# A planner takes the small loads of a recurrence as landing far later: a hybrid GDN and RWKV-7 encoder block on one core

## The chip, the core and the metric

The kernel runs on one core of a Trainium2 chip. The core has a matrix engine (PE, with its weight loads shown apart as PEld), a vector engine (DVE), a scalar engine (ACT), a general engine (POOL) and a sync engine (SP) from which most transfers are issued. Every engine works through its own list of instructions in order and waits on semaphores where it needs another engine or a transfer. The metric is the device time of one execution in microseconds, lower is better; the median of the runs is what is compared.

## The reference

One layer over 512 tokens of width 2048, in float32. What the change touches is the first half: the combined input projection and the two recurrent groups that are fed by it.

```python
xn = _rmsnorm(h, norm_mix)
y = xn @ w_in                       # 2048 -> 59 blocks of 128 columns
o_gdn = _gdn_group(y[..., :GDN_COLS], ...)      # 8 heads x 128, chunked gated delta rule
o_rwkv = _rwkv_group(y[..., GDN_COLS:], ...)    # 16 heads x 64, RWKV-7 scan
h = h + concat[o_gdn, o_rwkv] @ w_out
h = h + _cross_attention(_rmsnorm(h), _rmsnorm(mem), wq, wk, wv, wo)
h = h + square(relu(_rmsnorm(h) @ w_up)) @ w_down
out = _rmsnorm(h, norm_final)

# GDN, per head and chunk: a unit lower triangular system
M = where(strict, (k*beta) @ k.T * gamma, 0)
sol = triangular_solve(M + eye, [v*beta, k*beta*exp(G)])
# RWKV-7, per step
S = S * w_t + (S @ a_t) b_t^T + v_t k_t^T ;  o_t = S @ r_t
# its decay and its a come through low-rank products
w_log = -softplus(-(w0 + tanh(w_lo) @ w2)) - 0.5 ;  a = sigmoid(a0 + a_lo @ a2)
```

## The kernel before

**Precision and tiling.** Each float32 weight tile (128x1024, name `wraw`) is split into a rounded part `whi` (a cast on ACT) and a remainder `wlo` (a subtraction on DVE). Each 128x512 block of the projection then takes three products for each of 16 depth tiles: `xhi·whi`, `xlo·whi`, `xhi·wlo`. In the names of the trace, `py` are the accumulators of the 59 projection blocks, `kp` those of the cross-attention's key projection and `kq` those of a product behind it. Three `wraw` buffers, three `whi` and three `wlo` buffers rotate, and four buffers `y` take the finished blocks.

**The recurrence.** It is worked in eight rounds j = 0..7, each a pair of RWKV heads (function `rwkv(j)`) and one GDN head (`gdn(h)`). Each round needs seven projection blocks. In both groups a triangular inverse is wanted for each chunk. The function `inverse_blocks` inverts the 16x16 diagonal blocks on POOL and then turns them around through device memory: the masked products (`GA`, `GB` from `pgA`, `pgB`; for GDN `gEs`) are written to a scratch tensor `nd...`, read back as blocks (`sr` or `sgi`), inverted by some thirty small POOL operations, written to `bg16T`/`bg16U` (GDN: `bg8T`/`bg8U`), and loaded again in the layout that the PE wants: `r` and `E` for RWKV (`gk` and `gqn` for GDN). These last loads are the "turned-around blocks", lines 795 and 798. The PE products that use them first are `ri0x`, `ri1x` ... `ri7x` (RWKV) and `gi0x` ... `gi7x` (GDN); the number is the round. The other small load is `lw` (line 856), the low-rank weights of decay and a; its products are `pW` and `pA`, which open the next round.

**What sets the order.** The first half is not written in the order in which it runs. Each piece is a generator that yields operations; `run` keeps a clock for each engine and a table `landed` of when each tile is thought to be ready, takes the chain whose next operation can begin first (PE operations by that time alone, others with 150 ns for each step of their rank), and emits it. What is emitted is fixed: each engine then executes its list in that order. For a transfer, `issue` sets the time of landing to

```python
t, eng = max(state["dma"] + 700, t + 2900) + slack[1], "DMA"
```

where `slack[1]` is the `margin` of the `Lane` by which it was issued. The plain lane `SY` has a margin of 0, the lane `SL` holds the issue back instead (`wait`), and the lane `SM` is used at three places only: lines 795 and 798 (turned-around blocks) and 856 (`lw`). A reader of such a tile is not placed before the landing time, so a larger margin lets other chains, above all `projections()`, put their operations on the PE first.

**Side work.** Free DVE and DMA time of the first half is filled by `presums`: pieces of 410 columns of the MLP's down weights are loaded (`ds`), combined by four DVE operations and written back (`sd_s`). Whatever is not done by the last `kp` block is done later in other pieces.

Of the kernel before, what the change touches and what calls it, by code (L numbers as in the profile page):

```python
# [73 lines left out]
def build(tc, I, out):  # L74
    nc = tc.nc
# [128 lines left out]
                return self.key, nm, getattr(self.eng, nm), a, k, out, aps, self.slack  # L204
            return op

    SL, SM = Lane(nc.sync, "SP", wait=6000.0), Lane(nc.sync, "SP", margin=2500.0)
    DV, AC, GS, TE, SY = (Lane(e, k) for e, k in ((V, "DVE"), (S, "ACT"), (GP, "POOL"), (PE, "PE"), (nc.sync, "SP")))

    def cost(op):  # L210
# [168 lines left out]
    for n in range(2, NIN):  # L379
# [6 lines left out]
    Sd = {(e, m, j): pd.tile([P, 2048], F32, name=f"sd{e}_{m}_{j}", tag=f"sd{e}_{m}_{j}")  # L386
          for e, m in GROUPS for j in ("s1", "s2", "s3", "s4")}
# [1 line left out]
    todo = list(GROUPS)  # L389
    upto = {}  # L390

    def presum(e, m, c, n, d, Q=None):
        Q = Q or SY
        LD = Lane(nc.sync, "SP", margin=5000.0)
        tt = lambda o, a, b, op=ALU.subtract: DV.tensor_tensor(out=o, in0=a, in1=b, op=op)
        src = I["w_dm"][e, m]
        a11, a21, a22, a12 = b = [x[:, 0:n - c] for x in d]
        for i in (A21, A22, A11, A12):
            yield LD.dma_start(b[i], src[i][:, c:n])
        for j, op in (("s1", tt(a22, a21, a22, ALU.add)), ("s3", tt(a21, a11, a21)),  # L400
                      ("s2", tt(a11, a22, a11)), ("s4", tt(a12, a12, a11))):
            yield op
            yield Q.dma_start(Sd[e, m, j][:, c:n], op[5])
            upto[e, m, j] = upto.get((e, m, j), 0) + n - c

    def presums(d, width, stop):
        while todo and not stop():
            e, m = todo.pop(0)
            for c in range(0, 2048, width):
                if c and stop():  # L410
                    todo.insert(0, (e, m))
                    return
                yield from presum(e, m, c, min(c + width, 2048), d)

    hk = [("w", I["wk"][n][:, h * 1024:(h + 1) * 1024]) for n, h in kpo]
    wq += [("m", m) for m in mem4[:3]] + hk[:1] + [("m", mem4[3])] + hk[1:]
# [840 lines left out]
    def ahead():  # L1257
        yield after("rows")
        for j in range(NSET):
            chain(presums([tl(f"ds{j}{i}", PIECE, shape=[P, PIECE]) for i in range(4)], PIECE, after("kp", 15)),  # L1260
                  lambda eng: 2 if eng == "SP" else PRANK)
# [267 lines left out]
    for s in range(64):  # L1529
# [8 lines left out]
        if s > 1 and vsteps[s - 2][0] == "v" and vsteps[s - 2][2]:  # L1538
            n = vsteps[s - 2][1]
# [119 lines left out]
    for g in range(2):  # L1659
        banks = (("mm", 2), ("mg", 2), ("mg", 2), ("mm", 2)), (("scr", 1), ("scg", 1), ("mx", 2), ("mx", 2))  # L1660
        pts = [psb(f"sc{g}_{t}", *banks[g][t]) for t in range(4)]
        for n2 in range(8):
# [11 lines left out]
            for i, t in its:  # L1674
                n = 2 * n2 + i
# [88 lines left out]
    def take(lst):  # L1764
        yield lambda: bool(lst)
        return lst.pop(0)
# [8 lines left out]
    def tt(o, a, b, op=ALU.add):  # L1775
        return DV.tensor_tensor(out=o, in0=a, in1=b, op=op)
# [461 lines left out]
    def remaining():  # L2238
        left = [(e, m, c, min(c + 512, 2048)) for e, m in todo for c in range(upto.get((e, m, "s4"), 0), 2048, 512)]
        yield after("xd", 7)  # L2240
        chain(leftover(left, abfree, lambda d: True, after("ud", 26, 1)), lambda eng: 4)
        yield after("H", 3, 3)
        chain(leftover(left, [hp[7][:, i // 2, i % 2 * M:i % 2 * M + M] for i in range(4)], lambda d: True, after('ud', 30, 1), M), lambda eng: 4, ("spare7",))
        yield after("spare7")
        yield after("mul", units[33], B11, 0)
        for n in range(1):
            chain(leftover(left, cfree if n == 0 else abfree, lambda d: phase() in (1, 2, 3, 5) or phase() >= d), lambda eng: 4)

    def leftover(left, free, gate, stop=lambda: False, width=512):
        r = []  # L2250
        for _ in range(4):
            r.append((yield from take(free)))
        while left and not stop():
            yield lambda: not left or gate(left[0][0] // 2 * 2 + left[0][1])
            if left:
                e, m, c, n = left.pop(0)
                for c in range(c, n, width):
                    yield from presum(e, m, c, min(c + width, n), r, SY)
        free.extend(r)

    wf = []
# [139 lines left out]
```

## Time and profile before

| | before |
|---|---|
| time, median of 3 runs | 2932.04 us (2929.65 to 2935.57) |
| the profiled execution, its own time | 2930.33 us |
| its span, first to last instruction | 2928.2 us |
| mean granted PE clock | 0.995 |
| PE busy, 1000 to 2900 us | 1893 of 1900 us |
| DVE busy, first 1000 us | 753 us |
| ACT busy, first 1000 us | 541 us |
| POOL busy | 225.4 us |

The first half, with the projection and the recurrence, is the stretch from 0 to about 1010 us. A wait is listed with the engine that waited, the tile that it was about to write, what released it, the total in us, how many times, and the longest. A row of the table of stretches gives, after the bounds and the length, the busy time of PE, PEld, DVE, ACT and POOL with the instructions in brackets, then the granted PE clock as a share of full speed, the DMA share and GB/s. In a timeline a row gives start and duration, engine, line, operation, output and inputs, and in square brackets the idle time before it and what ended that.

### The profile page before, as it was taken

The numbers are of one execution on the slowest core, as the hardware profiler recorded it, in microseconds if no ns is written. First come the engines' busy times: TensorE is split into PE (matmuls) and PEld (weight loads), VectorE is DVE, ScalarE is ACT, GpSimd is POOL, SyncE is SP. The second block draws the span as 40 slices with busy tenths as digits, with TensorE's granted clock in tenths as the row PEclk, the third lists the DMA queues.
The fourth block names the chain that finished last, engine by engine and source line by source line (L and its number), as shares of the span: only waits on it lengthen the run. The fifth ranks groups of instructions, "written<-read, shape, count | busy, mean of one in ns | idle before, by whom it ended". The sixth has DMA issues, their size and how long they took to land. (4 is left out here: it accounts for less than half of the span.)

```text
span 2928.2 us, 49166 instructions
## 1 busy us (share of the span) xinstructions
PE 2877.8 (98%) x18794; PEld 2422.9 (83%) x18794; DVE 2331.5 (80%) x3551; ACT 1572.7 (54%) x2233; POOL 225.4 (8%) x547
## 2 busy tenths in 40 slices
PE   9999999999999999999999999999999999999998
PEld 7877777777877888879988888888888888888786
DVE  7787786786877876769955898888998878787998
ACT  6455554554555655664444655555555644454544
POOL 0213213213212100000000000000000000000000
PEclk9999999999999999999999999999999999999999
DMA  5646545555556588685423344655655878888633
GB/s 188 176 140 176 152 142 154 159 151 164 156 159 177 180 268 289 217 267 184 130 94 94 108 156 151 199 170 184 196 194 172 295 241 277 292 258 276 198 109 104
DMA packets 315451, 541.47 MB, mean 185 GB/s; under 512 B 101512, under 2 KB 184716, under 8 KB 315216
## 3 DMA queue, kind: packets, MB, share of 16 engines
q1 hardware_dynamic: 288976, 508.97, 56.2%
q10 hardware_dynamic: 26240, 29.37, 2.9%
q8 instruction: 147, 2.41, 0.3%
q14 instruction: 88, 0.72, 0.1%
HBM read 436.11 MB, written 102.12 MB: 184 GB/s over the span
## 5 line engine op out<-in xcount | busy, mean ns | idle before, releaser
L256 ACT CAST whi<-wraw 128x1024 fp32r<-128x1024 f32 (+1 forms) x364 | 381.6, 1049 | 436.8 <-PE py L256 163.2
L256 DVE TENSOR_TENSOR wlo<-wraw,whi 128x1024 fp32r<-128x1024 f32 (+1 forms) x364 | 446.3, 1227 | 114.6 <-ACT whi L256 102.9
L256 PE MATMUL py<-xhi,whi 128*128 128x512 f32 x928 | 374.9, 404 | 6.5 <-ACT xhi L256 6.5
L256 PE MATMUL py<-xlo,whi 128*128 128x512 f32 x928 | 376.4, 406 | 0.0
L256 PE MATMUL py<-xhi,wlo 128*128 128x512 f32 x928 | 374.6, 404 | 0.0
L256 ACT CAST whi<-w 128x1024 fp32r<-128x1024 f32 x181 | 190.5, 1054 | 220.0 <-PE mxu L256 47.3
L256 DVE TENSOR_TENSOR wlo<-w,whi 128x1024 fp32r<-128x1024 f32 x181 | 220.7, 1221 | 50.5 <-ACT whi L256 49.1
L256 PE MATMUL mxu<-cb,whi 128*128 128x512 f32 x1016 | 255.0, 392 | 0.0
L256 PEld LDWEIGHTS py<-xhi,whi 128*128 128x128 f32 x928 | 176.0, 190 | 41.3 <-ACT xhi L256 6.8
L256 PEld LDWEIGHTS mxu<-cb,whi 128*128 128x128 f32 x1016 | 182.8, 189 | 32.7
L256 PEld LDWEIGHTS py<-xlo,whi 128*128 128x128 f32 x928 | 176.0, 190 | 35.8 <-DVE xlo L256 1.4
L256 PEld LDWEIGHTS py<-xhi,wlo 128*128 128x128 f32 x928 | 176.2, 190 | 35.3 <-issue 1.8
L131 DVE TENSOR_TENSOR wlo<-wraw,whi 128x1024 fp32r<-128x1024 f32 x112 | 136.8, 1223 | 46.8 <-ACT whi L130 45.6
L130 ACT CAST whi<-wraw 128x1024 fp32r<-128x1024 f32 x112 | 117.8, 1053 | 88.3 <-PE op L122 25.7
L256 PEld LDWEIGHTS mxu<-cb,wlo 128*128 128x128 f32 x1016 | 138.7, 190 | 10.5 <-DVE wlo L256 0.7
L256 PE MATMUL mxu<-cb,wlo 128*128 128x256 f32 x1016 | 142.2, 282 | 0.3 <-DVE wlo L256 0.3
L256 PE MATMUL mgu<-cb,whi 128*128 128x512 f32 x512 | 129.4, 394 | 1.5 <-ACT whi L256 1.4
L256 PE MATMUL mxd<-whi,cb 128*128 128x512 f32 x512 | 127.0, 390 | 2.6 <-ACT whi L256 2.6
L256 PE MATMUL mgd<-whi,cb 128*128 128x512 f32 x512 | 126.4, 389 | 0.0
L256 ACT ACT_TABLE_LOAD x87 | 111.6, 1283 | 19.3 <-DVE suml_gn L256 11.5
L122 PE MATMUL op<-ob,whi 128*128 128x256 f32 (+1 forms) x752 | 115.3, 304 | 0.2 <-ACT whi L130 0.2
L256 PEld LDWEIGHTS mxd<-whi,cb 128*128 128x128 f32 x512 | 95.8, 188 | 23.7 <-ACT whi L256 3.5
(944 smaller groups left out, 6640.2 us busy)
## 6 DMA issues: line engine op xcount, KB each, us to landing
wraw<-in_w_in SPq DMA_DIRECT2D x116, 512.0 KB, 4.5
wraw<-in_w_up SPq DMA_DIRECT2D x65, 512.0 KB, 3.8
w<-in_w_up SPq DMA_DIRECT2D x63, 512.0 KB, 3.8
w<-sd_s SPq DMA_DIRECT2D x48, 512.0 KB, 5.8
wraw<-sd_s SPq DMA_DIRECT2D x48, 512.0 KB, 5.1
ds<-in_w_dm SPq DMA_DIRECT2D x116, 205.0 KB, 4.1
sd_s<-ds SPq DMA_DIRECT2D x116, 205.0 KB, 4.5
wraw<-in_w_dm SPq DMA_DIRECT2D x46, 512.0 KB, 5.4
```

Source lines behind the costliest of these rows:

```text
L122: PE.matmul(o, l, r, start=start, stop=stop, skip_group_check=again)
L130: S.copy(hi, src)
L131: V.tensor_tensor(out=lo, in0=src, in1=hi.bitcast(F32), op=ALU.subtract)
L256: f(*a, **k)
```

## The change

The margin of the lane `SM` goes from 2500 to 8000 ns. The rest of the diff passes the lanes of `presum` as arguments: the load lane keeps its margin of 5000, the store lane keeps 0, so these lines set the same values as before.

```diff
--- before
+++ after
@@ -204,7 +204,7 @@
                 return self.key, nm, getattr(self.eng, nm), a, k, out, aps, self.slack
             return op
 
-    SL, SM = Lane(nc.sync, "SP", wait=6000.0), Lane(nc.sync, "SP", margin=2500.0)
+    SL, SM = Lane(nc.sync, "SP", wait=6000.0), Lane(nc.sync, "SP", margin=8000.0)
     DV, AC, GS, TE, SY = (Lane(e, k) for e, k in ((V, "DVE"), (S, "ACT"), (GP, "POOL"), (PE, "PE"), (nc.sync, "SP")))
 
     def cost(op):
@@ -389,9 +389,7 @@
     todo = list(GROUPS)
     upto = {}
 
-    def presum(e, m, c, n, d, Q=None):
-        Q = Q or SY
-        LD = Lane(nc.sync, "SP", margin=5000.0)
+    def presum(e, m, c, n, d, LD=Lane(nc.sync, "SP", margin=5000.0), ST=SY):
         tt = lambda o, a, b, op=ALU.subtract: DV.tensor_tensor(out=o, in0=a, in1=b, op=op)
         src = I["w_dm"][e, m]
         a11, a21, a22, a12 = b = [x[:, 0:n - c] for x in d]
@@ -400,7 +398,7 @@
         for j, op in (("s1", tt(a22, a21, a22, ALU.add)), ("s3", tt(a21, a11, a21)),
                       ("s2", tt(a11, a22, a11)), ("s4", tt(a12, a12, a11))):
             yield op
-            yield Q.dma_start(Sd[e, m, j][:, c:n], op[5])
+            yield ST.dma_start(Sd[e, m, j][:, c:n], op[5])
             upto[e, m, j] = upto.get((e, m, j), 0) + n - c
 
     def presums(d, width, stop):
@@ -410,7 +408,7 @@
                 if c and stop():
                     todo.insert(0, (e, m))
                     return
-                yield from presum(e, m, c, min(c + width, 2048), d)
+                yield from presum(e, m, c, min(c + width, 2048), d, Lane(nc.sync, "SP", margin=5000.0), Lane(nc.sync, "SP", 0.0, 0.0))
 
     hk = [("w", I["wk"][n][:, h * 1024:(h + 1) * 1024]) for n, h in kpo]
     wq += [("m", m) for m in mem4[:3]] + hk[:1] + [("m", mem4[3])] + hk[1:]
@@ -2255,7 +2253,7 @@
             if left:
                 e, m, c, n = left.pop(0)
                 for c in range(c, n, width):
-                    yield from presum(e, m, c, min(c + width, n), r, SY)
+                    yield from presum(e, m, c, min(c + width, n), r)
         free.extend(r)
 
     wf = []
```

The numbers of instructions in the first half's matrix work stay as they are. What changes is the order, at nearly every place after round 0. Three places follow; a name's last number only tells buffers apart.

The first place is the PE list at round 2, just ahead of the first product that uses the turned-around block `r` (`ri2x`). Before:

```order
L256 MATMUL py_3876<-xhi_354,whi_3815 128x512
L256 MATMUL py_3876<-xlo_355,whi_3815 128x512
L256 MATMUL py_3876<-xhi_354,wlo_3816 128x512
L256 MATMUL py_3876<-xhi_365,whi_3815 128x512
L256 MATMUL pkk_3937<-gk_3927,gkn_3909 128x128
L256 MATMUL ri2x_3915<-r_3843,GA_3509 64x64
L256 MATMUL ri2x_3915<-r_3843,GB_3510 64x64
```

Now:

```order
L256 MATMUL py_3965<-xhi_316,wlo_3663 128x512
L256 MATMUL py_3965<-xhi_343,whi_3758 128x512
L256 MATMUL py_3965<-xlo_344,whi_3758 128x512
L256 MATMUL pkk_4005<-gk_3999,gkn_3984 128x128 x4
L256 MATMUL py_3965<-xhi_343,wlo_3759 128x512
L256 MATMUL ri2x_3947<-r_3869,GA_3558 64x64
L256 MATMUL ri2x_3947<-r_3869,GB_3559 64x64
```

All four `pkk` products now stand ahead of `ri2x` instead of one, and the projection has gone on into the next block's first half. Counted from the last product of the round's `pgA`/`pgB` (which starts the way of the block through POOL and memory) to its first `ri` product, the projection products (`py` or `kp`, 128x512) in between are, for rounds 1 to 7: before 107, 111, 109, 111, 109, 106, 109; now 131, 126, 128, 128, 128, 135, 117 (and 8 of 128x256).

The second place is SP's list at round 7, around the stores to `bg16T`/`bg16U` and the loads from them; `wraw` from `in_wk` is the first weight tile of the key projection. Before:

```order
L256 DMA wraw_10298<-in_memT 128x1024
L256 DMA bg16T<-sr_10046 64x16x16
L256 DMA bg16U<-sr_10046 64x16x16
L256 DMA r_10305<-bg16T 64x8x64 x2
L256 DMA E_564_10306<-bg16U 64x4x64 x4
L256 DMA sd_0_s_150<-ds_55_825 128x410
L256 DMA wraw_10386<-in_wk 128x1024
```

Now:

```order
L256 DMA ds_56_826<-in_w_dm 128x410
L256 DMA bg16T<-sr_10126 64x16x16
L256 DMA bg16U<-sr_10126 64x16x16
L256 DMA wraw_10405<-in_wk 128x1024
L256 DMA r_10386<-bg16T 64x8x64 x2
L256 DMA E_565_10387<-bg16U 64x4x64 x4
L256 DMA wraw_10442<-in_memT 128x1024
```

The weight tile from `in_wk` now stands ahead of the six loads from `bg16T` and `bg16U`, where it stood behind them.

The third place is SP's list at round 6, the same stores and loads. Before:

```order
L256 DMA bg16T<-sr_8733 64x16x16
L256 DMA bg16U<-sr_8733 64x16x16
L256 DMA ds_56_826<-in_w_dm 128x410
L256 DMA wraw_9007<-in_w_in 128x1024
L256 DMA r_8991<-bg16T 64x8x64 x2
L256 DMA E_495_8992<-bg16U 64x4x64 x4
```

Now:

```order
L256 DMA bg16T<-sr_8843 64x16x16
L256 DMA bg16U<-sr_8843 64x16x16
L256 DMA wraw_9104<-in_w_in 128x1024
L256 DMA ds_56_826<-in_w_dm 128x410
L256 DMA wraw_9139<-in_w_in 128x1024
L256 DMA r_9106<-bg16T 64x8x64 x2
L256 DMA E_496_9107<-bg16U 64x4x64 x4
```

Two weight tiles and a `ds` piece stand between the store and the load, where one weight tile and a `ds` piece stood. In rounds 1 and 7 one weight tile now stands there, in rounds 4 and 5 three small loads of `lg`. Over the whole first half 39 instead of 36 `presum` pieces (of 410 or 408 columns) are worked, so fewer are left for later.

## The prediction

> **What bounds the kernel now.** I read the page first: which engine has no room.
>
> ```profile
> span 2928.2 us, 49166 instructions
> PE 2877.8 (98%) x18794; PEld 2422.9 (83%) x18794; DVE 2331.5 (80%) x3551; ACT 1572.7 (54%) x2233; POOL 225.4 (8%) x547
> ```
>
> PE is busy for 2877.8 of 2928.2 us, so the change can win little beyond the 50.4 us in which PE sits idle, plus what a lower clock costs. Next, PE's waits in the first 1020 us, which hold every place that the change can reach (tile about to be written, releaser, total, times, longest; the very first wait, for the first inputs, is left out):
>
> ```profile
> PE ri6x L256 <- DMA r<-bg16T: 4.2, 2, 3.9
> PE ri2x L256 <- DMA r<-bg16T: 3.2, 2, 3.0
> PE ri5x L256 <- DMA r<-bg16T: 3.1, 2, 2.5
> PE kp L256 <- ACT whi L256: 3.1, 1, 3.1
> PE pW L256 <- DMA lw<-in_w2a: 2.4, 2, 2.1
> PE ri3x L256 <- DMA r<-bg16T: 2.1, 2, 1.6
> PE ri4x L256 <- DMA r<-bg16T: 1.9, 2, 1.5
> PE gn L256 <- DVE suml_gn L256: 1.5, 2, 1.1
> PE pwt L256 <- issue: 1.0, 1, 1.0
> PE kp L256 <- DVE wlo L256: 0.5, 1, 0.5
> ```
>
> The reader should see that the two kinds of load in the change are the releasers of most of it: the turned-around `r` in rounds 2 to 6 (4.2 + 3.2 + 3.1 + 2.1 + 1.9 = 14.5 us) and `lw` (2.4 us). The GDN loads `gk` and `gqn` release no wait at all. Third view, the stretches of 20 us around these waits, for the granted clock (the fourth number from the end, before DMA share and GB/s):
>
> ```profile
> 340.00:360.00 20.00, 16.76 (x156) 13.52 (x154) 10.85 (x18) 7.60 (x9) 6.70 (x14) 0.91 0.63 166
> 460.00:480.00 20.00, 17.88 (x255) 14.16 (x253) 12.65 (x21) 5.67 (x8) 5.47 (x11) 1.00 0.53 123
> 580.00:600.00 20.00, 19.02 (x306) 15.05 (x306) 12.72 (x26) 7.60 (x15) 2.21 (x7) 0.91 0.77 207
> 680.00:700.00 20.00, 16.91 (x103) 13.77 (x104) 10.69 (x14) 8.71 (x10) 11.97 (x28) 0.97 0.46 116
> 700.00:720.00 20.00, 20.00 (x282) 15.68 (x282) 11.14 (x21) 10.62 (x18) 9.48 (x26) 0.94 0.67 189
> 800.00:820.00 20.00, 15.83 (x151) 12.78 (x151) 12.53 (x18) 8.00 (x9) 4.83 (x13) 0.91 0.80 196
> 920.00:940.00 20.00, 16.45 (x93) 12.83 (x94) 13.54 (x27) 12.57 (x23) 0.00 (x0) 0.86 0.71 186
> 940.00:960.00 20.00, 20.00 (x307) 17.03 (x306) 14.89 (x24) 11.21 (x20) 4.33 (x11) 0.97 0.55 164
> ```
>
> After four of the five waits for `r` the clock falls, and PE then works slower on whatever is ready. The timeline of PE shows it: two products at 127 us, where nothing waits, then the wait of round 4 and two products behind it.
>
> ```profile
> 127.68 0.39 PE L256 MATMUL py<-xhi,whi 128*128 128x512 f32 x1
> 127.91 0.39 PE L256 MATMUL py<-xlo,whi 128*128 128x512 f32 x1
> ...
> 580.53 0.29 PE L256 MATMUL ri4x<-r,GA 64*64 64x64 f32 x2 [1.49 <-DMA r<-bg16T]
> 581.27 0.27 PE L256 MATMUL ri4x<-r,GB 64*64 64x64 f32 x1 [0.45 <-DMA r<-bg16T]
> ...
> 582.93 0.63 PE L256 MATMUL py<-xhi,wlo 128*128 128x512 f32 x1
> 583.36 0.63 PE L256 MATMUL py<-xhi,whi 128*128 128x512 f32 x1
> ```
>
> Projection products start 0.23 us apart at full clock, 0.43 us apart here.
>
> **The change part by part.** *Removed: the waits for `r`.* Why is PE early? The planner counts 2.9 us from issue to landing plus 2.5 us of margin, but on the chip the way through SP is longer. Round 4, SP's issues:
>
> ```profile
> 574.97 0.58 SPq L256 DMA_DIRECT2D bg16T<-sr  x1
> 577.53 1.27 SPq L256 DMA_DIRECT2D r<-bg16T  x2
> ```
>
> The load leaves 577.53 us and PE gets it at 580.53 and 581.27 us. The new order puts 15, 19, 17, 19 and 29 more projection products into this way in rounds 2 to 6 (the counts 111, 109, 111, 109, 106 and 126, 128, 128, 128, 135 of the section on the change). At 0.23 us each that is 3.4, 4.4, 3.9, 4.4 and 6.7 us against waits of 3.2, 2.1, 1.9, 3.1 and 4.2 us. Each is covered; round 2 by least, but there three more `pkk` products also move ahead of `ri2x`, and this row has eight passes, four products:
>
> ```profile
> 129.88 1.05 PE L256 MATMUL pkk<-gk,gkn 128*128 128x128 f32 x8
> ```
>
> Three of them give up to 0.8 us more. So the gain is 14.5 us; bounds 0 (the load moves as much as its use) and 14.5 us.
>
> *Removed: the wait for `lw`.* Its use moves behind more projection work as well (between `pwt` of round 1 and `pW` of round 2 there are 48 projection products in the new order, 22 in the old, 6 us more against a wait of at most 2.1 us). Gain 2.4 us, bounds 0 and 2.4.
>
> *Removed with them: the slow clock.* Deficit times length: 0.09 x 20 = 1.8 us each in 340 to 360, 580 to 600 and 800 to 820, and 0.6 + 1.2 = 1.8 us in 680 to 720. Sum 7.2 us. The wait of round 3, at 460 to 480, cost none. Bounds: 0 (other short gaps keep the clock down) and 7.2; I take 7.2, since the stretches without a gap stand at 1.00.
>
> The Trainium skill, "TensorE: Matmul & The Clock Gate", section "Part 1: The HAM clock gate", says that the clock drops to half only after an idle window of about 3.4 us. By that rule only the 4.2 us of round 6 would have cost clock, this term would be 1.8 instead of 7.2 us, and the sum 5.4 us poorer; the trace differs, for 1.49 + 0.45 us of idle in round 4 were followed by 0.91.
>
> *Moved: the first weight tile of the key projection.* In round 7, SP and ACT before:
>
> ```profile
> 917.35 0.58 SPq L256 DMA_DIRECT2D bg16T<-sr  x1
> 918.02 0.62 SPq L256 DMA_DIRECT2D bg16U<-sr  x1
> 922.48 1.27 SPq L256 DMA_DIRECT2D r<-bg16T  x2
> 927.10 0.43 SPq L256 DMA_DIRECT2D wraw<-in_wk  x1
> ...
> 933.89 1.05 ACT L256 CAST whi<-wraw 128x1024 fp32r<-128x1024 f32 x1 [5.28 <-DMA wraw<-in_wk]
> ```
>
> SP stands still from 918.6 to 922.5 us for the stores to land, and the tile from `in_wk` leaves only after `r` and `E`; ACT waits 5.28 us for it, PE 3.1 + 0.5 us, and the clock then costs 2.8 + 0.6 us (920 to 960). In the new order this tile leaves ahead of `r`, up to 927.1 - 918.7 = 8.4 us sooner. Bounds: 0, and 3.6 + 3.4 = 7.0 us. I take 5, since nothing but SP's place made it late, yet its own buffer may be the next limit.
>
> *Added: the recurrence runs some 45 projection products later in the middle rounds.* This could cost at the end, but it does not add up: in the new order the first products of `ri2x` to `ri6x` come 43 to 74 projection products later, those of `ri7x` 32, and the last inverse product of the last GDN head comes 12 *earlier*, counted in projection products. `kq`, which must wait for that inverse, begins after 3346 of them in both orders, more than 100 later, so there the delay is hidden behind `kp` products; without these it would cost 45 x 0.23 = 10 us.
>
> *Added: new short waits.* Every round has dozens of steps from PE over DVE or ACT back to PE, laid closely by the planner. Nearest rows: the `gn` and `pwt` waits, 1.5 + 1.0 us in all of the first half, for which I count no gain. New ones are bounded by 0 and by one wait of 1.5 us in each of eight rounds, 12 us. I take 5, nearer the rows.
>
> *The three extra `presum` pieces* are twelve DVE operations on an engine that works 12.5 to 18 of 20 us here; they come off the later part, where PE's list is the same row for row. I put them at nothing; if DVE were full, this row gives 12 x 0.58 = 7 us:
>
> ```profile
> 513.49 0.58 DVE L256 TENSOR_TENSOR ds<-ds,ds 128x410 f32<-128x410 f32 x1
> ```
>
> **Sum.** -14.5 - 2.4 - 7.2 - 5 + 5 = -24.1 us. The profiled execution took 2930.33 us (2.1 of it around the span), so 2906.2; it ran 1.7 below the median of 2932.04, so 2907.9, say **2908 us**. With no new wait and all of the key-projection term it is 2901; with neither that term nor luck (12 us of new waits) 2920. That is this case's own range.
>
> **The rivals.** *The waits only move* (no change). The cover put ahead of `r` is taken from steps behind it: from `pW` to the next `pn` there were 16 to 22 us of PE work, now mostly 11 to 12, estimated from the products in the order at the start distances above. If in each round DVE and ACT are 2 us late there, and every second such wait costs 1.8 us of clock, that is 16 + 7.2 = 23.2 us in place of the 5 taken: 2908 - 5 + 23 = 2926, and with the key-projection wait kept, 2931. For it: DVE is the second busiest engine, and recurrence and GDN levels now meet more closely. Against it: so far these steps made only 2.5 us of waits.
>
> *Half of it comes* (faster, but less). The loads are covered, but the clock recovers only for round 6 and the key projection waits as before: -14.5 - 2.4 - 1.8 + 5 = -13.7, so 2918 us. For it: short gaps remain. Against it: the 1.00 rows.
>
> *SP blocks the loads* (slower). SP issues in order, and weight tiles now stand between the store to `bg16T` and the load from it in rounds 1, 6 and 7. Such a tile's issue waits until DVE has finished reading its buffer:
>
> ```profile
> SPq L256 <- DVE wlo L256: 731.2, 294, 11.6
> ```
>
> The mean is 2.5 us, the longest 11.6. At the mean the cover holds; where the wait exceeds the cover left (6.7 - 4.2 = 2.5 us in round 6, about as much in 1 and 7) PE stands. At 11.6 us it stands 9 us in each of three rounds, with 1.8 us of clock: 32.4 us. The gains left (rounds 2 to 5: 10.3, `lw` 2.4, clock 5.4) are 18.1, so +14.3: 2946 us. Against it: round 6 already had one weight tile at that place, and its wait for `r`, 4.2 us, is the only sign of it.
>
> *The change does nothing* can be set aside: PE's list differs from round 0 on.
>
> **How the numbers follow.** Main case 0.60, half of it 0.14, waits only move 0.13, SP blocks 0.13. Within 0.2% means within 5.9 us of 2932.0. Faster: 0.60 + 0.14 and 0.01 of the third = 0.75; same 0.12; slower 0.13. The range runs from 2898 (a little under the best sum, 2901) to 2936, which holds the first three cases and leaves out the blocked SP.
>
> **What would show it.** Right: no `PE ri.x <- DMA r<-bg16T` rows of more than 0.5 us among PE's waits, none for `lw`, no stretch below 0.95 from 100 to 900 us, `kp` without a wait for `whi`, and the last product of the first half some 24 us sooner. Wrong: new rows of PE waiting for DVE or ACT that sum to over 10 us, or SP's waits for `wlo` just ahead of an `r` load, with `ri1x`, `ri6x` or `ri7x` waiting on it.

## The result and the profile after

| | before | after |
|---|---|---|
| time, median | 2933.4 us (2929.65 to 2935.57) | 2911.98 us (2910.92 to 2913.18, 4 runs) |
| the profiled execution, its own time | 2930.33 us | 2911.43 us |
| its span | 2928.2 us | 2909.6 us |
| first `kq` product, the end of the first half | 1051.3 us | 1034.8 us |
| mean granted PE clock | 0.995 | 0.997 |

The ratio is 0.9928, 95% interval 0.9911 to 0.9946: about 21 us faster. The runs of before beside the changed kernel have a median of 2933.4 us instead of 2932.04. The profiled executions differ by 18.9 us, of which 16.5 lie ahead of the first `kq` product. The page of the changed kernel begins:

```profile
span 2909.6 us, 49187 instructions
PE 2874.6 (99%) x18794; PEld 2420.8 (83%) x18794; DVE 2331.9 (80%) x3547; ACT 1573.0 (54%) x2233; POOL 225.8 (8%) x547
```

PE does the same 18794 products in nearly the same busy time; what went is idle time and time at a low clock. PE's waits from 0 to 1020 us after the change (tile, releaser, total, times, longest):

```profile
PE py L256 <- ACT xhi L256: 8.0, 1, 8.0
PE gn L256 <- DVE suml_gn L256: 2.2, 4, 0.7
PE pkk L256 <- DVE gk L256: 2.2, 1, 2.2
PE kp L256 <- ACT whi L256: 1.2, 1, 1.2
PE kp L256 <- DVE wlo L256: 1.1, 2, 0.8
PE rs L256 <- DVE Qs L256: 0.7, 1, 0.7
PE gi3x L256 <- DMA gk<-bg8T: 0.5, 2, 0.3
PE pak L256 <- ACT BK L256: 0.3, 1, 0.3
PE pal L256 <- ACT kp L256: 0.2, 1, 0.2
```

No row names `r` or `lw` any more. The first row is the wait for the first inputs, before anything that the change reaches; it is 1.5 us longer than in the profile of before (6.5), and it was 6.4 to 8.0 us in the profiles of this study. Without it PE waits 8.4 us instead of 23.1. The stretches of 20 us (the granted clock is the third number from the end, not the fourth as the prediction says):

```profile
340.00:360.00 20.00, 19.37 (x171) 15.65 (x170) 13.61 (x22) 11.04 (x15) 9.17 (x20) 1.00 0.70 163
580.00:600.00 20.00, 20.00 (x319) 15.92 (x318) 15.06 (x25) 10.46 (x16) 2.92 (x8) 1.00 0.84 232
800.00:820.00 20.00, 20.00 (x207) 16.05 (x205) 15.70 (x24) 11.13 (x13) 3.03 (x9) 1.00 0.87 209
900.00:920.00 20.00, 17.44 (x122) 14.16 (x115) 10.78 (x20) 12.05 (x22) 9.73 (x27) 0.92 0.69 168
```

The dips at 340, 580, 680 to 720 and 800 us are gone. One is left, at 900 to 920 us, around the start of the key projection.

### The profile page after: what moved, and what is told of

It reads as the page before. It is cut to its first block, busy times and chain, and to the rows that moved or that the text cites. A ratio compares the mean times of both kernels' runs of the same rounds, so it can differ in the third digit from the quotient of the medians.

```text
span 2909.6 us, 49187 instructions
## 1 busy us (share of the span) xinstructions
PE 2874.6 (99%) x18794; PEld 2420.8 (83%) x18794; DVE 2331.9 (80%) x3547; ACT 1573.0 (54%) x2233; POOL 225.8 (8%) x547
## 4 chain that ended last, share of the span: by engine, by line
PE 94%; DMA 2%; DVE 2%; ACT 1%; issue 1%; POOL 0%; SPq 0%; ACTq 0%; DVEq 0%; POOLq 0%
PE py L256 21%; PE mxu L256 12%; PE mgu L256 6%; PE mgd L256 6%; PE mxd L256 6%; PE op L122 5%; PE vp L122 3%; PE kq L256 3%; PE kp L256 3%; PE sc L122 3%; PE at L122 3%; PE scgd L256 3%; PE scrd L256 3%; PE mmu L256 3%; PE mmd L256 3%; PE vo L122 2%
```

## The experiments

Twelve runs were made in three groups; those of a group and the runs of before beside them share a chip. Times are compared within a group.

| group | kernel | median, us | ratio to before, 95% interval |
|---|---|---|---|
| 1 | before | 2927.74 | |
| 1 | margin 4000 | 2906.73 | 0.9928 [0.9913, 0.9943] |
| 1 | margin 5500 | 2914.70 | 0.9957 [0.9940, 0.9974] |
| 1 | margin 12000 | 2931.57 | 1.0008 [0.9997, 1.0019] |
| 1 | 8000 for `r`, `E` alone | 2910.79 | 0.9939 [0.9923, 0.9955] |
| 2 | before | 2929.10 | |
| 2 | the change | 2910.06 | 0.9934 [0.9919, 0.9948] |
| 2 | 8000 for `lw` alone | 2920.20 | 0.9970 [0.9958, 0.9983] |
| 2 | 8000 for the GDN blocks alone | 2929.09 | 1.0002 [0.9990, 1.0013] |
| 2 | before with short `ds` loads | 2914.40 | 0.9946 [0.9930, 0.9961] |
| 3 | before | 2928.26 | |
| 3 | the change | 2910.49 | 0.9941 [0.9927, 0.9955] |
| 3 | the change, weight tile earlier | 2912.71 | 0.9949 [0.9936, 0.9961] |
| 3 | margin 4000 | 2910.78 | 0.9941 [0.9928, 0.9953] |
| 3 | margin 4000, weight tile earlier | 2910.82 | 0.9942 [0.9930, 0.9954] |

### How much margin: 4000, 5500, 12000

```diff
-    SL, SM = Lane(nc.sync, "SP", wait=6000.0), Lane(nc.sync, "SP", margin=8000.0)
+    SL, SM = Lane(nc.sync, "SP", wait=6000.0), Lane(nc.sync, "SP", margin=4000.0)
```

and the same with 5500 and 12000.

> Margin 4000 for all three small loads. Theory A (the gain is the covered waits): the order puts 113, 114, 114, 114, 122 projection products ahead of ri2x to ri6x, where 111 + 14, 109 + 9, 111 + 9, 109 + 14, 106 + 18 would cover the old waits; about 5 us of waits for r are left, mostly in rounds 2 and 5, with two clock drops of 1.8 us. So about 12 to 15 us faster than before, 2918 to 2922. Theory B (the gain comes from the new order as such, with three more presum pieces and fewer changes between kinds of products): 40 presum pieces are worked here, more than the 39 of the change, so all of the gain is there, 2912.

> Margin 5500. Theory A: covers of 119, 119, 119, 119, 133 products leave 1 to 2 us of waits for r, in rounds 2 and 5; lw covered. 2912 to 2917, within 0.2% of the change. Theory B: the same, 2912. This run sets where the curve flattens.

> Margin 12000. Theory A: rounds 2 to 5 have covers of 146, 143, 149, 144 products, far more than the loads need, so nothing is won there over the change; in round 6 only 69 products are left ahead of ri6x (135 in the change), so PE must stand some (124 - 69) x 0.23 = 12 us there, and the time is 2920 to 2928, slower than the change. Theory B: 44 presum pieces, at least as fast as the change, 2912 or less.

Margin 4000: PE's waits from 0 to 1040 us, after the one for the first inputs:

```profile
PE gn L256 <- DVE suml_gn L256: 1.6, 2, 1.1
PE ri7t L256 <- DVE k L256: 1.4, 1, 1.4
PE ri7s L256 <- DVE k L256: 0.9, 1, 0.9
```

No wait for `r` is left, although only 113 or 114 projection products stand ahead of `ri2x` to `ri5x` and 122 ahead of `ri6x`, where before had 111, 109, 111, 109 and 106. In rounds 2 to 5 these are two to five products more, at 0.23 us at most 1.2 us, against waits of 3.2, 2.1, 1.9 and 3.1 us, so cover alone does not account for it; theory A, which went by cover alone, expected 5 us of waits and 2918 to 2922 us. The section on the hardware comes back to that. A margin of 5500 has no such wait either; its 2.7 us wait at `ri7s` and 4.7 us at `gn` are of the kind that stands next in line.

Margin 12000: the way of `r` is covered by 143 to 152 products in rounds 0 to 5, and nothing waits for it, but the time is that of before. PE's waits, and the two longest of them in its timeline:

```profile
PE gn L256 <- DVE suml_gn L256: 11.8, 5, 7.2
PE pkk L256 <- DVE gk L256: 6.5, 2, 4.2
PE ri7t L256 <- DVE k L256: 2.4, 1, 2.4
```

```profile
808.77 0.39 PE L256 MATMUL py<-xhi,wlo 128*128 128x512 f32 x1
816.35 0.80 PE L256 MATMUL gn<-suml_gn,onesr 128*128 128x512 f32 x1 [7.19 <-DVE suml_gn L256]
...
821.80 2.08 PE L256 MATMUL pkk<-gk,gkn 128*128 128x128 f32 x8 [4.23 <-DVE gk L256]
```

Here the rival "the waits only move" is seen in full. Projection products are the filler for every step that goes over DVE and ACT. Ahead of their first `ri` product rounds 0 to 5 each take 34 to 45 more of them than before; in round 6 only 69 are left ahead of `ri6x`, and eight between the recurrence's `pkv` and the GDN's `gn`. There PE stands 7.2 us and, after `gn`, 4.2 us more. The granted clock is 0.82 and 0.84 from 800 to 840 us. With 44 `presum` pieces worked, theory B, by which the pieces carry the gain, expected 2912 us or less, and so it falls.

### Which of the loads: `r` and `E`, `lw`, the GDN blocks

```diff
+    SR, SG, SW = (Lane(nc.sync, "SP", margin=m) for m in (8000.0, 2500.0, 2500.0))
...
+        SB = SR if nm[0] == "r" else SG
...
-                    yield SM.dma_start(dst[HALF[z]], full[:, z * n:z * n + n, :])
+                    yield SB.dma_start(dst[HALF[z]], full[:, z * n:z * n + n, :])
...
-        yield SM.dma_start(lw, I["w2a2"][:, js])
+        yield SW.dma_start(lw, I["w2a2"][:, js])
```

The load of `E` takes `SB` likewise. The second kernel has (2500, 2500, 8000), that is `lw` alone, the third (2500, 8000, 2500), the GDN blocks alone. The change itself ran beside the last two.

> Margin 8000 for the turned-around blocks of RWKV (r, E) alone; those of GDN and lw stay at 2500. Theory A: covers of 127 and more in rounds 1 to 6, so the waits for r (14.5 us) and their clock (7.2 us) are gone and lw may still wait up to 2.4 us: 2911 to 2917. Theory C (the loads of GDN or lw carry a part of it): more than 8 us slower than the change, over 2920.

> Margin 8000 for lw alone. Theory A (covered waits): lw never waits again (2.4 us), but the covers of r stay at 103 to 117 products, so PE waits for r as before, about 14 us, with the clock drops: 0 to 5 us faster than before. Theory D (any new order is as good as another, since the loads in front of r are then issued and land sooner, as in the run with margin 4000 where they did by 3 to 5 us in rounds 2 to 5): the waits for r shrink to under 7 us and the time is 10 us or more faster than before.

> Margin 8000 for the GDN blocks alone, which nothing waited for. Theory A: covers of r at 106 to 117 products, waits for r as before or 2 to 3 us less, and the last inverse stands only just ahead of kq: within 8 us of before. Theory D: 10 us or more faster than before.

> The change once more, on the chip of the following runs. 0.9928 of before, so about 20 us faster; its profile is the yardstick for them.

The RWKV blocks alone bring as much as the change can be told from: 0.9939, no wait for `r`, 0.6 us for `lw`. `lw` alone brings 0.9970, some 9 us, more than the 2.4 us of its own wait: the waits for `r` fell from 14.5 to 8.9 us although nothing was asked of them. The order is another one from there on, and in rounds 4 and 5, where the wait is gone, the load of `r` leaves SP 25.6 and 26.5 us after the last `pgA`/`pgB` product instead of 30.1 and 31.0. Neither theory holds as it stands: A left the waits as they were, D had them under 7 us and the gain at 10 us or more. The parts do not add up, 17 + 9 + 0 against 19.

The GDN blocks alone bring nothing, and four rows of PE's waits from 0 to 1100 us show where the cover is missing then:

```profile
PE gi7u L257 <- DVE gkn L257: 5.4, 2, 2.9
PE pW L257 <- DMA lw<-in_w2a: 4.1, 3, 2.3
PE ri6x L257 <- DMA r<-bg16T: 1.9, 2, 1.4
PE gi7u L257 <- DVE TtG L257: 1.5, 2, 0.8
```

The waits for `r` fell here too, to 4.2 us. But the last GDN inverse (`gi7u`) now reaches the end of the key projection: in the order its last product stands behind all 3344 `py` and `kp` products that come ahead of `kq` (the prediction counted 3346), where before had it after 3220 and the change after 3208. With no `kp` product left to fill, its steps over DVE show, 6.9 us. This is the cost that the prediction named for "without these" `kp` products. With `lw` alone the last `gi7u` stands behind all of them too, but the first `gi7x` comes there after 3270 of them and not after 3319, and PE waits only 1.2 us, at `gs`, behind it.

### The order of before, with less traffic

The order of PE and SP stays that of before; nearly all `ds` loads of the first half bring 16 of their 410 columns, 8 KB instead of 205 KB each. The kernel leaves out the rest of these weights, so its output is not that of the layer, and only its time counts.

```diff
             op = LD.dma_start(b[i], src[i][:, c:n])
+            if manual_on[0] and len(upto) >= 4 and n - c > 16:
+                full, cut = op[2], (b[i][:, 0:16], src[i][:, c:c + 16])
+                op = op[:2] + (lambda *_, full=full, cut=cut: full(*cut),) + op[3:]
+            yield op
```

> The kernel before with the same order on every engine, but nearly all presum loads of the first half bring 16 columns instead of 410 (the old columns of the buffers are combined and stored instead, so the down weights' sums are other numbers). Theory D (r comes late because the load of its blocks, sr, stands behind the presum transfers): sr lands 2.8 us after its issue in all rounds instead of 2.7 to 8.4, the store to bg16T leaves 22 to 24 us after the last pg product instead of 27 to 28 in rounds 2 to 5, the waits for r fall below 5 us and the time by 10 us or more. Theory A alone (only the place of the use counts): waits for r of 12 us or more, time within 5 us of before.

The ratio is 0.9946, three quarters of what the change brings beside it, without one product moved. PE's waits for `r` from 0 to 1040 us:

```profile
PE ri4x L256 <- DMA r<-bg16T: 2.0, 2, 1.4
PE ri2x L256 <- DMA r<-bg16T: 1.1, 2, 0.8
PE ri6x L256 <- DMA r<-bg16T: 0.9, 2, 0.6
PE ri3x L256 <- DMA r<-bg16T: 0.6, 1, 0.6
PE ri5x L256 <- DMA r<-bg16T: 0.6, 1, 0.6
```

They sum to 5.2 us instead of 14.5, and the wait for `lw` is gone. So a good part of the lateness of `r` in the kernel before is other traffic. Theory D holds in the time; the waits end just over its 5 us, and `sr` does not land in 2.8 us in all rounds, as the section on the hardware shows. `kq` starts at 1035.1 us, as with the change beside it (1034.4): the same wait can be removed by covering the load or by letting it land sooner.

### The first weight tile of the key projection

```diff
-    wq += [("m", m) for m in mem4[:3]] + hk[:1] + [("m", mem4[3])] + hk[1:]
+    wq += [("m", m) for m in mem4[:2]] + hk[:1] + [("m", m) for m in mem4[2:]] + hk[1:]
```

This was laid on the change and on margin 4000, with both of these beside them.

> The change once more, as the measure for the three kernels beside it on the same chip. Every theory: 0.993 to 0.994 of the kernel before, about 2910 to 2912 us, with the waits of the key projection's place still there (pkk for gk about 2.2 us, kp for whi and wlo together 2.3 to 3.1 us).

> The change with one more edit: the key projection's first weight tile takes the place of the third memory tile in the order of the raw buffers, and leaves SP at about 895 us instead of 910.6. PE's list is the same up to the middle of round 7's key-projection products. Theory A (the rest of the key-projection wait is the tile's place behind the bg16T store): the waits of kp for whi and wlo, 2.3 us, go; the wait of pkk for gk, 2.2 us, stays or shrinks; with 0 to 1.6 us of clock the kernel is 2 to 4 us faster than the change beside it, up to 6 if the pkk wait goes too. Rival B (DVE and ACT, with the memory tiles to be scaled, are the limit at that place): the wait moves to the next kp products or to the ri7 steps, and the time stays within 1 us of the change.

> A margin of 4000 again, now beside the change on one chip. Theory E (a few products of cover are enough, since the blocks also land 3 to 5 us earlier in the new orders, and more cover only opens waits elsewhere): 3 to 5 us faster than the change, 2906 to 2908 us. Rival F (the two are alike and the 5 us between them earlier were the chip): within 1 us of the change. Rival G (less cover leaves waits for r in other executions): slower than the change, with rows of PE waiting for r.

> A margin of 4000 with the early weight tile of the key projection. With 4000 the key projection did not wait for its tile in the earlier profile (ri7 products stand ahead of it), and the clock fell to 0.84 from 900 to 920 us after waits of ri7s, ri7t and ri7w, 2.9 us together. Theory A: kp products now stand ahead of the ri7 steps, these waits go, and it is 2 to 5 us faster than 4000 alone. Rival B: the waits only change their name, within 1 us of 4000 alone.

On the change the tile now leaves SP at 893.85 us, 14 us ahead of the store to `bg16T`. PE's timeline from 905 to 935 us then has these waits:

```profile
913.93 0.50 PE L256 MATMUL kp<-mhl,wlo 128*128 128x256 f32 x2 [0.79 <-DVE wlo L256]
...
922.38 0.80 PE L256 MATMUL kp<-mhl,whi 128*128 128x512 f32 x1 [4.98 <-ACT whi L256]
...
923.64 0.80 PE L256 MATMUL kp<-mhl,wlo 128*128 128x256 f32 x2 [0.47 <-DVE wlo L256]
```

The change beside it, same stretch:

```profile
914.58 1.16 PE L256 MATMUL pkk<-gk,gkn 128*128 128x128 f32 x8 [2.17 <-DVE gk L256]
...
921.91 0.50 PE L256 MATMUL kp<-mhl,whi 128*128 128x512 f32 x1 [2.43 <-ACT whi L256]
...
923.17 0.50 PE L256 MATMUL kp<-mhl,wlo 128*128 128x256 f32 x2 [0.76 <-DVE wlo L256]
```

The `kp` waits at about 922 us stand, in both, ahead of the 17th and 18th `kp` product, the first that use the second weight tile: the change beside it had no wait for its first tile any more, so there was nothing of that to win. The `pkk` wait goes, and what it gave comes back in front of the second tile: 0.79 + 4.98 + 0.47 = 6.2 us against 2.17 + 2.43 + 0.76 = 5.4, with the second tile's products at 922.4 and 921.9 us. Theory A falls. Rival B holds in kind, though the time is 2.2 us longer (2912.71 against 2910.49 us) where it allowed 1. ACT shows why:

```profile
918.71 1.70 ACT L256 ACTIVATE mhl<-wraw,prm 128x256 fp32r<-128x256 f32 x4 [3.04 <-DMA wraw<-in_memT]
921.28 1.04 ACT L256 CAST whi<-wraw 128x1024 fp32r<-128x1024 f32 x1 [0.87 <-DMA wraw<-in_wk]
```

The last memory tile and the second weight tile follow the loads of `r` and `E` on SP, and ACT waits for each of them to land. The place of the first tile is not what limits here.

On margin 4000 the edit changes nothing that can be told (2910.82 and 2910.78 us): the `ri7` waits are gone, and a wait of 3.3 us of `kp` for `whi` stands in their place. And margin 4000 itself, 2906.73 us in the first group, is level with the change when both run on one chip: rival F holds. Its second profile has no wait for `r` either, but 3.3 us for `lw`, where the first had 0.4. No kernel of the study is shown to beat the change. Margins of 4000 and 8000 are level, and 2500 and 12000 are slower; 5500, which never ran beside the change, came out 8 us slower than 4000 on one chip, so the stretch between them is not shown to be flat.

## Why the prediction was right

The forecast was 2908 us, a sum of -24.1 us on the profiled execution; it came to -18.9. Its signs came in part: the rows for `r` and `lw` are gone, no dip stands before 900 us, and new waits for DVE and ACT stay under 10 us; but `kp` still waits for `whi`, and the first half ends 16.5 us sooner, not 24. Term by term:

**The waits for `r`, -14.5.** All of it came; the largest wait of before, 3.9 us in round 6, has no successor. The reason given, cover, is only half of the matter: margin 4000 removes the same waits with little of that cover, and the short `ds` loads remove 9.3 us of 14.5 with none.

**The wait for `lw`, -2.4.** Came in full.

**The slow clock, -7.2.** Came nearly in full, mechanism and size. Stretches of 3.4 us of before show what a dip is (PE's busy time and instructions, granted clock, DMA share, GB/s); in each pair the first row holds the end of the wait for `r`, in rounds 2, 3 and 6, and the second follows it:

```profile
350.74:354.15 3.41, 1.73 (x39) 1.00 0.82 145
354.16:357.56 3.40, 3.40 (x45) 0.50 0.87 308
466.80:470.21 3.41, 2.13 (x37) 1.00 0.63 126
470.21:473.62 3.41, 3.41 (x73) 1.00 0.92 244
808.13:811.54 3.41, 0.34 (x6) 1.00 1.21 237
811.55:814.95 3.40, 3.40 (x36) 0.50 1.00 288
```

Behind rounds 2 and 6 the clock is at 0.50 for 3.4 us, PE is busy all the while, and so a dip costs up to 1.7 us; the four dips behind `r` come to 6.8 us. Counted product by product, against the median distance of the same pair of products elsewhere, they come to 6.9. It is not the projection alone that is slow there: the pairs of `ri2s` products stand 0.11 us apart at 356.5 us, the pairs of `ri3s` 0.06 us apart at 471.2. By the rule of the Trainium skill, "TensorE: Matmul & The Clock Gate", section "Part 1: The HAM clock gate" (an idle window of about 3.4 us before the clock drops), only the round with a wait of 3.9 us would have given anything; the trace differs, for in the 3.4 us ahead of the dips at 354, 583 and 699 us PE was busy for 1.73, 1.86 and 1.28 us, and these dips went with their waits of 3.0, 1.5 and 2.5 us.

**The key projection, -5.** This term was mis-sized: it gave about -0.5. The waits there went from 3.6 to 2.2 + 1.2 + 1.1 = 4.5 us, and the time at 0.50 went from 6.8 us, 5.8 of them busy, to 3.4 us, 3.0 of them busy, which is worth some 1.4 us. What the prediction said of SP is so; after the change:

```profile
909.25 0.58 SPq L256 DMA_DIRECT2D bg16T<-sr  x1
909.93 0.62 SPq L256 DMA_DIRECT2D bg16U<-sr  x1
910.64 0.61 SPq L256 DMA_DIRECT2D wraw<-in_wk  x1
911.78 1.28 SPq L256 DMA_DIRECT2D r<-bg16T  x2
```

The tile leaves 1.4 us after the store instead of 9.8, and the wait for this tile falls from 3.6 to 0.4 us. PE's waits at the place after the change are others:

```profile
915.84 1.32 PE L256 MATMUL pkk<-gk,gkn 128*128 128x128 f32 x8 [2.17 <-DVE gk L256]
...
917.97 0.79 PE L256 MATMUL kp<-mhl,wlo 128*128 128x256 f32 x2 [0.38 <-DVE wlo L256]
...
923.80 0.50 PE L256 MATMUL kp<-mhl,whi 128*128 128x512 f32 x1 [1.22 <-ACT whi L256]
925.06 0.50 PE L256 MATMUL kp<-mhl,wlo 128*128 128x256 f32 x2 [0.76 <-DVE wlo L256]
```

The step that failed is to count the end of this wait as time won because "nothing but SP's place made it late". PE came to the place some 18 us earlier as well (the last `py` product at 913.3 instead of 931.5 us), `pkk`, now ahead of `kp`, waits for DVE, and the rows at 923.80 and 925.06 are the second weight tile. The early tile then showed the same: with the first tile in hand PE waits for the second. The bounds of 0 and 7.0 held for the gain; the value taken between them did not.

**New short waits, +5.** Listed ones: `gn` 0.7 more, `rs`, `gi3x`, `pak` and `pal` 1.7 together, the 1.0 us at `pwt` gone, so +1.4. Another +4.8 is what the balance below leaves over. So the size is near, but by another way than the one forecast: most of it lies below what the list of waits shows. The short products, the 64-wide steps of the recurrence and GDN mostly, took 230.8 instead of 227.3 us from start to next start with the listed waits taken off, although some of them had run at half clock before. Which of their steps it is was not settled.

**The balance of the first half**: waits for `r` -14.5 and `lw` -2.4, their clock -6.8, the key projection -0.5, listed new waits +1.4, the longer wait for the first inputs +1.5; that is -21.3 against -16.5 measured, so +4.8 is left over. Another 2.1 us came between `kq` and the end of the span, 0.6 of it a wait of `kq` and 0.8 in `vo`; the prediction had put the later part at nothing.

**The rivals.** "The waits only move" did not happen at 8000 and does at 12000. "SP blocks the loads" did not happen: with one and two weight tiles between store and load, `ri1x`, `ri6x` and `ri7x` have no wait. "Half of it comes" (-13.7) is as near in size as the main case, 5.2 us off either way, but not in kind: its two conditions were a clock that recovers only once, which is refuted, and the key projection waiting as before, which is nearly so.

## What to carry to other kernels

Where a planner sets the order, its estimate for one kind of load is a dial for how much filler stands ahead of the use. Filler is one stock for all steps: look for what stands next in line without it, and for the last link, which has none behind it. When a wait for a load is found, ask first why the load is late, since removing traffic ahead of it can be worth nearly as much as covering it. Price a short wait with the clock behind it: here 14.5 us of waits had 6.8 us of slow clock with them. When one wait of a tile sequence is removed, price the next tile of the sequence before counting the gain.

## What the hardware showed that was not expected

Whether a short wait costs clock depends on where it falls. All five dips of before start a whole number of steps of 3.413 us apart (354.15 to 582.85 us is 67 steps), and each follows a step in which PE was busy for 0.10 to 0.55 of the time. The wait of round 3 (1.6 + 0.5 us) was no shorter than that of round 4 (1.49 + 0.45 us), but in its steps PE stayed busy for 0.76 and 0.62 of the time, and the clock stayed at 1.00. Over all profiles of this study, a drop from full clock came behind steps that were busy up to 0.57, never above; between 0.49 and 0.57 it came behind some and not behind others.

A small load's way depends on what goes with it. The load of `sr` in round 3, of some 64 KB, and the first POOL operation that uses it; before, then after:

```profile
440.89 0.60 SPq L256 DMA_DIRECT2D sr<-ndri  x1
...
448.63 0.41 POOL L256 TENSOR_TENSOR sr<-sr 64x15 f32<-64x15 f32 x1 [26.64 <-ACT BK L256]
```

```profile
440.85 0.59 SPq L256 DMA_DIRECT2D sr<-ndri  x1
...
444.52 0.21 POOL L256 TENSOR_TENSOR sr<-sr 64x15 f32<-64x15 f32 x1 [21.27 <-DVE wlo L256]
```

That is 7.7 us before and 3.7 us after (the releaser in brackets is long done, so the load is what POOL waited for). Over the eight rounds it is 2.7 to 8.4 us before, 2.8 to 6.6 after, and 2.7 to 2.8 with a margin of 4000 in all rounds but one (3.5). With it the store to `bg16T` leaves 27.2 to 28.5 us after the last `pgA`/`pgB` product in rounds 2 to 5 of before, 23.7 to 23.9 after the change, 21.9 to 23.9 at margin 4000. The load of `r` leaves 2.7 to 5.8 us sooner in these two orders. With margin 4000 that is 3.5 to 5.8 us, more than the waits of 1.9 to 3.2 us that before had in these rounds, and this is why 114 products were cover enough; in the change the load leaves 2.7 to 3.8 us sooner and is used later as well. With the short `ds` loads the store comes at 24.8 to 26.9 us in these rounds, so bytes are part of the cause; `sr` still took 7.2 and 6.5 us in rounds 3 and 5 there, and which transfer holds it then stays open.
